# A fused low-rank update in fp16 on one core: A and B moved into SyncE's load queue, w laid out by ScalarE, stores released by turns

## The chip, the core and the metric

The kernel runs on one core of a Trainium2 chip. The metric is device time in microseconds. A profile shows one execution: the span from its first to its last instruction on the core, the busy times of the engines, and the transfers. PE is TensorE, DVE is VectorE, ACT is ScalarE, POOL is GpSimd and SP is SyncE, which only issues transfers here.

## What is computed

```python
batch, seq, d_model, r = 16, 512, 768, 16
x = np.random.randn(batch, seq, d_model).astype(np.float32)
A = np.random.randn(d_model, r).astype(np.float32) * 0.1
B = np.random.randn(r, d_model).astype(np.float32) * 0.1
scale = 0.5

def reference(x, A, B, scale):
    lora = np.matmul(np.matmul(x, A), B)
    return (x + scale * lora).astype(np.float32)
```

x and the output have 8192 rows of 768 fp32 numbers, 25.17 MB each. A and B have 48 KB each.

## The kernel before

The 8192 rows are 64 tiles of 128 rows. They are cut into six parts of 2, 6, 8, 16, 16 and 16 tiles (`PARTS`). Three rooms in SBUF of 16 tiles each (`rooms`) hold x; the last part takes the room of the first three parts again, so its two loads wait until the stores of those have landed. Seven transfers load x (`LOADS`, in tiles: 2, 6, 8, 16, 16, 8, 8) and seven with the same cuts store the result from the same place (`STORES`).

Work goes by groups of 8 tiles, eight in all, numbered here from 0. For each group:

1. ScalarE casts the first 4 tiles to fp16 into `xh` and GpSimd the other 4 (`narrowed`, L158).
2. VectorE turns each half in blocks of 32x32 (`turned`, L233), so that the 768 columns come to lie on partitions.
3. TensorE multiplies by `w_bd`, a layout of A, in 24 steps of 256 columns (`projected`, L261), into `y_ps`.
4. ScalarE scales the four blocks of the result into `y_bd` (`spread`, L197).
5. TensorE multiplies by `b_mm`, a layout of B, two tiles at a time (`raised`, L275), into the two PSUM buffers `lora`.
6. VectorE adds a pair of tiles of `lora` to x in place (L243), 4 additions a group. When the group is the last that a store needs, it drains and counts up `s_sum` (L247).

TensorE interleaves: group h's projection runs in three thirds, between the pairs of the group before. In its first round the pairs are empty runs, whose results nobody adds. VectorE turns group g+1 ahead of adding group g.

`xh`, `y_bd`, `y_ps` and `lora` have two buffers. Every engine has its own program, in the order written, and waits on semaphores. `s_free` counts lora buffers that VectorE has added, `s_lora` those that TensorE has filled, `s_y` finished projections.

The start: GpSimd clears `b_rows`, `pick`, `w_bd` and both `y_bd`; VectorE clears `a_rows` (L209). ScalarE issues the transfers of B (L180) and A (L184) on its own queue, each after the clearing of its target. ScalarE casts B (L189), TensorE spreads it over the partitions with `pick` (L285), and ScalarE copies the result to `b_mm` (L191). VectorE transposes A (L211), gathers it into `w_one` (L218, three copies) and copies that to the four diagonal blocks of `w_bd` (L226).

SyncE's program is the queue of x: five loads (L134), then the stores of parts 0 to 2 (L138), each after a wait on `s_sum`, then the last two loads, each after a wait for stores that have landed, then the other four stores.

Of the kernel before, what the change touches and what calls it, by code (L numbers as in the profile page):

```python
# [22 lines left out]
APART = 8  # L23
# [3 lines left out]
def kernel(  # L27
# [11 lines left out]
    Q = 32  # L39
    NQ = P // Q  # L40
# [4 lines left out]
    R = A.shape[1]  # L45
    NC = D // 64
    NG = sum(PARTS) // GROUP
    PAIRS = GROUP // 2
# [15 lines left out]
    a_rows = sb("a_rows", [P, 64 * R], fp32)  # L64
    a_t = sb("a_t", [P, 2, R, Q], fp32)
    w_one = sb("w_one", [Q, NC, 2, R], MM_DT)
    b_rows = sb("b_rows", [P, D], fp32)
    b_half = sb("b_half", [P, D], MM_DT)
    pick = sb("pick", [P, NQ, Q], MM_DT)
    w_bd = sb("w_bd", [P, NC, 2, P], MM_DT)  # L70
    b_mm = sb("b_mm", [P, D], MM_DT)
    xh = [sb(f"xh{i}", [P, GROUP, D], MM_DT) for i in range(2)]
    y_bd = [sb(f"y_bd{i}", [P, GROUP, P], MM_DT) for i in range(2)]
    lora = [ps(f"lora_ps{i}", [P, 2, D]) for i in range(2)]
# [4 lines left out]
    def sem(name):  # L79
        sems.append(nc.alloc_semaphore(name))  # L80
        return sems[-1]
# [18 lines left out]
    LOADS = [(0, 0, 2), (1, 0, 6), (2, 0, 8), (3, 0, 16), (4, 0, 16), (5, 0, 8), (5, 8, 8)]  # L100
# [5 lines left out]

    s_a, s_b = sem("s_a"), sem("s_b")
    s_brows, s_pick, s_bh, s_bp = sem("s_brows"), sem("s_pick"), sem("s_bh"), sem("s_bp")
    s_ready, s_zero, s_w, s_bm = sem("s_ready"), sem("s_zero"), sem("s_w"), sem("s_bm")
    s_nact, s_npool = sem("s_nact"), sem("s_npool")  # L110
    s_turned, s_y, s_spread = sem("s_turned"), sem("s_y"), sem("s_spread")
    s_lora, s_free, s_sum = sem("s_lora"), sem("s_free"), sem("s_sum")
# [18 lines left out]
    @block.sync  # L131
    def _(e):
        def load(ld):
            e.dma_start(out=held(*ld), in_=memory(x2, *ld)).then_inc(s_load[ld], 16)  # L134

        def store(st, done):
            e.wait_ge(s_sum, STORED.index(groups_for(*st)) + 1)
            e.dma_start(out=memory(out2, *st), in_=held(*st)).then_inc(done, 16)  # L138

        load(LOADS[0])  # L140
        for ld in LOADS[1:5]:
            load(ld)
        for st, done in zip(STORES, (s_out0, s_out0, s_out1)):
            store(st, done)
        e.wait_ge(s_out0, 32)
        load(LOADS[5])
        e.wait_ge(s_out1, 16)
        load(LOADS[6])
        for st in STORES[3:]:
            store(st, s_out)  # L150

    def narrowed(e, copy, done, g, q):
        t = g * GROUP + q * SUB
        for s in dict.fromkeys(load_sem(t + k) for k in range(SUB)):
            e.wait_ge(s, 16)
        if g >= 2:
            e.wait_ge(s_y, g - 1)
        copy(  # L158
            out=xh[g % 2][:, ds(q * SUB, SUB), :], in_=held(*where[t], SUB)
        ).then_inc(done, 1)  # L160

    @block.gpsimd
    def _(e):
        e.memset(b_rows, 0.0).then_inc(s_brows, 1)  # L164
        e.memset(pick, 0.0).then_inc(s_pick, 1)
        e.memset(w_bd.rearrange("p c k m -> p (c k m)").bitcast(fp32), 0.0)  # L166
        for t in y_bd:
            e.memset(t.rearrange("p s m -> p (s m)").bitcast(fp32), 0.0)  # L168
        e.wait_ge(s_pick, 1)
        e.affine_select(  # L170
            out=pick, in_=pick, compare_op=mybir.AluOpType.not_equal, fill=1.0, base=0,
            pattern=[[0, NQ], [-APART, Q]], channel_multiplier=1,
        ).then_inc(s_zero, 1)
        for g in range(NG):
            narrowed(e, e.tensor_copy, s_npool, g, 1)

    @block.scalar
    def _(e):
        e.wait_ge(s_brows, 1)
        e.dma_start(  # L180
            out=b_rows[0 : R * APART : APART, :], in_=B
        ).then_inc(s_b, 16)
        e.wait_ge(s_ready, 1)
        e.dma_start(  # L184
            out=a_rows[0 : NC * APART : APART, :],
            in_=A.rearrange("(c e) r -> c (e r)", e=64),
        ).then_inc(s_a, 16)
        e.wait_ge(s_b, 16)
        e.copy(out=b_half, in_=b_rows).then_inc(s_bh, 1)  # L189
        e.wait_ge(s_bp, 1)  # L190
        e.copy(out=b_mm, in_=lora[0][:, 0, :]).then_inc(s_bm, 1)  # L191

        def spread(g):
            e.wait_ge(s_y, g + 1)
            for b in range(NQ):
                q = ds(b * Q, Q)
                last = e.mul(out=y_bd[g % 2][q, :, q], in_=y_ps[g % 2][q, :, :], mul=sc)  # L197
            last.then_inc(s_spread, 1)

        narrowed(e, e.copy, s_nact, 0, 0)  # L200
        narrowed(e, e.copy, s_nact, 1, 0)
        for g in range(NG):
            spread(g)
            if g + 2 < NG:
                narrowed(e, e.copy, s_nact, g + 2, 0)

    @block.vector
    def _(e):
        e.memset(a_rows, 0.0).then_inc(s_ready, 1)  # L209
        e.wait_ge(s_a, 16)  # L210
        e.transpose(  # L211
            out=a_t[0 : NC * APART].rearrange("i k r c -> i (k r) c"),
            in_=a_rows[0 : NC * APART].rearrange("c (i k r) -> c (k r) i", k=2, r=R),
        ).then_inc(s_ready, 1)
        e.wait_ge(s_ready, 2)
        EACH = Q // APART
        for b in range(NC // EACH):
            last = e.tensor_copy(  # L218
                out=w_one[:, ds(b * EACH, EACH), :, :],
                in_=a_t[ds(b * Q, Q)].rearrange("i k r (c n) -> i c k r n", n=APART)[..., 0],  # L220
            )
        last.then_inc(s_ready, 1)
        e.wait_ge(s_ready, 3)
        e.wait_ge(s_zero, 1)
        for b in range(NQ):
            last = e.tensor_copy(out=w_bd[ds(b * Q, Q), :, :, ds(b * Q, R)], in_=w_one)  # L226
        last.then_inc(s_w, 1)

        def turned(g):
            for q, s in ((0, s_nact), (1, s_npool)):  # L230
                e.wait_ge(s, g + 1)
                v = xh[g % 2][:, ds(q * SUB, SUB), :].bitcast(fp32)
                last = e.transpose(out=v, in_=v)  # L233
            last.then_inc(s_turned, 1)

        turned(0)
        for g in range(NG):
            if g + 1 < NG:
                turned(g + 1)
            for p in range(PAIRS):  # L240
                xs = held(*where[g * GROUP + 2 * p], 2)
                e.wait_ge(s_lora, (g + 1) * PAIRS + p + 1)
                e.tensor_tensor(  # L243
                    out=xs, in0=xs, in1=lora[p % 2], op=mybir.AluOpType.add
                ).then_inc(s_free, 1)
            if g + 1 in STORED:
                e.drain().then_inc(s_sum, 1)  # L247

    @block.tensor
    def _(e):  # L250
        def take(s):
            e.wait_ge(s, 1)
            e.sem_inc(s, -1)  # L253

        def projected(h, steps):
            if steps[0] == 0:
                take(s_turned)
            xv = xh[h].rearrange("p s (c j k) -> p s c j k", c=NC, k=2)
            for m in steps:
                c, k = divmod(m, 2)  # L260
                last = e.matmul(  # L261
                    y_ps[h], w_bd[:, c, k, :], xv[:, :, c, :, k],
                    start=(m == 0), stop=(m == MMS - 1),
                )
            if steps[-1] == MMS - 1:
                last.then_inc(s_y, 1)

        def raised(h, p):
            if p == 0:
                take(s_spread)  # L270
            take(s_free)
            t = lora[p % 2]
            for k in range(2):
                for n0, w in ((0, 512), (512, 256)) if k == 0 else ((0, 256), (256, 512)):
                    last = e.matmul(  # L275
                        t[:, k, ds(n0, w)], y_bd[h][:, 2 * p + k, :], b_mm[:, ds(n0, w)],
                        start=True, stop=True,
                    )
            last.then_inc(s_lora, 1)


        e.wait_ge(s_bh, 1)
        e.wait_ge(s_zero, 1)
        for n0, w in ((0, 512), (512, 256)):
            last = e.matmul(  # L285
                lora[0][:, 0, ds(n0, w)], pick.rearrange("p b r -> p (b r)"),
                b_half[:, ds(n0, w)], start=True, stop=True,
            )
        last.then_inc(s_bp, 1)
        e.sem_inc(s_spread, 1)  # L290
        e.sem_inc(s_free, 2 + PAIRS)
        e.wait_ge(s_w, 1)
        e.wait_ge(s_bm, 1)
        with e.Fori(0, NG // 2):
            for h in range(2):
                raised(1 - h, 0)
                raised(1 - h, 1)
                projected(h, range(0, THIRD))
                raised(1 - h, 2)
                projected(h, range(THIRD, 2 * THIRD))  # L300
                raised(1 - h, 3)
                projected(h, range(2 * THIRD, MMS))
        for p in range(PAIRS):
            raised(1, p)
# [43 lines left out]
```

## Time and profile before

| what | value |
|---|---|
| time, median of 3 runs | 124.71 us (124.66 to 126.03) |
| profiled execution | 124.84 us, its span 122.93 us |
| busy: VectorE | 87.0 us, 71% of the span |
| busy: TensorE matmuls / weight loads | 53.9 us / 31.8 us |
| busy: ScalarE / GpSimd | 36.9 us / 25.6 us |
| moved | 50.46 MB, 410 GB/s over the span |
| queue q1 (SyncE's) | 50.33 MB, 96.5% of 16 DMA engines' span |
| queue q10 (ScalarE's) | 0.10 MB, 0.2% |
| B, issue to landing | 6.9 us |
| mean granted TensorE clock | 0.899 |

Times in the timeline count from the first instruction of the span. A group's line gives the code line, engine, operation, output and inputs with their shapes, how many there were, the busy time and the mean of one, and the idle time before them with what ended it. A wait of several semaphores is put down to the one that came last. In a table of stretches, a packet is booked in the stretch in which it starts or ends, so the DMA share of a short stretch can be over 1.

### The profile page before, as it was taken

To read this page: it belongs to the slowest core of one execution; us is meant where nothing else is said; L and a number is where in the kernel's file an instruction comes from. 1 tells how busy PE (TensorE), PEld (TensorE's weight loads), DVE (VectorE), ACT (ScalarE), POOL (GpSimd) and SP (SyncE) were. 2 spreads that over 40 slices of the span, in tenths; PEclk is the share of its full clock that TensorE was granted. 3 is DMA by queue.
4 is the path that set the end of the run, shared out by engine and by line. 5 is a ranking of instruction groups with operands and counts; after the bars stand their busy time and mean duration, and the time that the engine had idled before them with its cause. 6 is when DMAs were issued, how large, how long until landed. Compare 5 with 4: busy or idle time off the path is not lost. (4 is left out here: it accounts for less than half of the span.)

```text
span 122.9 us, 967 instructions
## 1 busy us (share of the span) xinstructions
PE 53.9 (44%) x338; PEld 31.8 (26%) x338; DVE 87.0 (71%) x57; ACT 36.9 (30%) x43; POOL 25.6 (21%) x18
## 2 busy tenths in 40 slices
PE   0002068768306994493483477449438353000000
PEld 0000034445103562262242254236225221000000
DVE  2006993959729989999999999999999789300000
ACT  0416608220199106708504082640400400000000
POOL 7402608000196001708000080440000000000000
PEclk9999999999995599999999999999999999555555
DMA  3999999799799795999999999999899799799990
GB/s 98 429 415 450 416 528 432 336 512 480 304 496 496 320 464 228 490 418 432 456 392 464 432 400 480 400 496 448 352 480 496 336 464 466 325 456 400 456 440 40
DMA packets 2074, 50.46 MB, mean 410 GB/s; under 512 B 252, under 2 KB 252, under 8 KB 536
## 3 DMA queue, kind: packets, MB, share of 16 engines
q1 hardware_dynamic: 2016, 50.33, 96.5%
q10 hardware_dynamic: 56, 0.10, 0.2%
q8 instruction: 1, 0.02, 0.0%
q14 instruction: 1, 0.01, 0.0%
HBM read 25.26 MB, written 25.17 MB: 410 GB/s over the span
## 5 line engine op out<-in xcount | busy, mean ns | idle before, releaser
L243 DVE TENSOR_TENSOR x_sb<-x_sb,lora_ps 128x1536 f32<-128x1536 f32 x32 | 53.8, 1740 | 3.5 <-PE lora_ps L275 3.5
L275 PE MATMUL lora_ps<-b_mm,y_bd 128*128 128x512 f16 (+1 forms) x144 | 30.9, 351 | 30.8 <-PEq L253 30.8
L158 POOL CAST xh<-x_sb 128x3072 f16<-128x3072 f32 x8 | 21.9, 2746 | 55.0 <-DMA x_sb<-in_x_dram 50.5
L233 DVE STREAM_TRANSPOSE xh<-xh 128x1536 f32<-128x1536 f32 x16 | 27.5, 1755 | 5.4 <-ACT xh L158 5.0
L261 PE MATMUL ps_yt<-xh,w_bd 128*128 128x256 f16 x192 | 26.1, 277 | 9.0 <-PEq L253 9.0
L158 ACT CAST xh<-x_sb 128x3072 f16<-128x3072 f32 x8 | 22.0, 2752 | 18.2 <-DMA x_sb<-in_x_dram 18.2
L275 PEld LDWEIGHTS lora_ps<-b_mm,y_bd 128*128 128x128 f16 x144 | 13.2, 102 | 44.6 <-issue 38.9
L261 PEld LDWEIGHTS ps_yt<-xh,w_bd 128*128 128x128 f16 x192 | 18.4, 98 | 16.9 <-issue 12.0
L197 ACT ACTIVATE y_bd<-ps_yt 32x256 f16<-32x256 f32 x32 | 12.0, 374 | 34.3 <-PE ps_yt L261 34.0
L211 DVE STREAM_TRANSPOSE a_t<-a_rows 96x1024 f32<-96x1024 f32 x1 | 1.9, 1926 | 8.3 <-DMA a_rows<-in_A_dram 8.3
L285 PE MATMUL lora_ps<-b_half,pick 128*128 128x512 f16 (+1 forms) x2 | 0.8, 514 | 9.6 <-ACT b_half L189 9.6
L285 PEld LDWEIGHTS lora_ps<-b_half,pick 128*128 128x128 f16 x2 | 0.1, 110 | 9.6 <-ACT b_half L189 9.6
L218 DVE CAST w_one<-a_t 32x128 f16<-32x128 f32 x3 | 2.5, 836 | 0.1
L189 ACT ACT_TABLE_LOAD x1 | 1.3, 1283 | 3.7 <-issue 3.7
L189 ACT CAST b_half<-b_rows 128x768 f16<-128x768 f32 x1 | 0.8, 832 | 3.7 <-DMA b_rows<-in_B_dram 3.7
L209 DVE MEMSET a_rows<- 128x1024 f32 x1 | 0.9, 912 | 1.2 <-SPq L127 1.2
L166 POOL MEMSET w_bd<- 128x1536 f32 x1 | 1.4, 1382 | 0.0
L191 ACT CAST b_mm<-lora_ps 128x768 f16<-128x768 f32 x1 | 0.8, 798 | 0.9 <-PE lora_ps L285 0.9
L226 DVE COPY w_bd<-w_one 32x384 f16<-32x384 f16 x4 | 1.0, 251 | 0.1
L168 POOL MEMSET y_bd<- 128x512 f32 x2 | 1.0, 524 | 0.0
L164 POOL MEMSET b_rows<- 128x768 f32 x1 | 0.7, 737 | 0.5 <-SPq L127 0.5
L170 POOL TENSOR_SCALAR_AFFINE_SELECT pick<-pick 128x128 f16<-128x128 f16 x1 | 0.3, 309 | 0.0
(5 smaller groups left out, 0.6 us busy)
## 6 DMA issues: line engine op xcount, KB each, us to landing
x_sb<-in_x_dram SPq DMA_DIRECT2D x2, 6144.0 KB, 38.1
out_dram<-x_sb SPq DMA_DIRECT2D x2, 6144.0 KB, 22.9
x_sb<-in_x_dram SPq DMA_DIRECT2D x3, 3072.0 KB, 15.1
out_dram<-x_sb SPq DMA_DIRECT2D x3, 3072.0 KB, 16.4
x_sb<-in_x_dram SPq DMA_DIRECT2D x1, 2304.0 KB, 10.1
out_dram<-x_sb SPq DMA_DIRECT2D x1, 2304.0 KB, 22.3
x_sb<-in_x_dram SPq DMA_DIRECT2D x1, 768.0 KB, 4.5
out_dram<-x_sb SPq DMA_DIRECT2D x1, 768.0 KB, 17.2
```

The costliest lines, as they stand in the source:

```text
L158: copy(out=xh[g % 2][:, ds(q * SUB, SUB), :], in_=held(*where[t], SUB)).then_inc(done, 1)
L166: e.memset(w_bd.rearrange("p c k m -> p (c k m)").bitcast(fp32), 0.0)
L168: e.memset(t.rearrange("p s m -> p (s m)").bitcast(fp32), 0.0)
L189: e.copy(out=b_half, in_=b_rows).then_inc(s_bh, 1)
L197: last = e.mul(out=y_bd[g % 2][q, :, q], in_=y_ps[g % 2][q, :, :], mul=sc)
L211: e.transpose(out=a_t[0 : NC * APART].rearrange("i k r c -> i (k r) c"), in_=a_rows[0 : NC * APART].rearrange("c (i k r) -> c (k r) i", k= ...
L218: last = e.tensor_copy(out=w_one[:, ds(b * EACH, EACH), :, :], in_=a_t[ds(b * Q, Q)].rearrange("i k r (c n) -> i c k r n", n=APART)[..., 0],)
L226: last = e.tensor_copy(out=w_bd[ds(b * Q, Q), :, :, ds(b * Q, R)], in_=w_one)
L233: last = e.transpose(out=v, in_=v)
L243: e.tensor_tensor(out=xs, in0=xs, in1=lora[p % 2], op=mybir.AluOpType.add).then_inc(s_free, 1)
L261: last = e.matmul(y_ps[h], w_bd[:, c, k, :], xv[:, :, c, :, k], start=(m == 0), stop=(m == MMS - 1),)
L275: last = e.matmul(t[:, k, ds(n0, w)], y_bd[h][:, 2 * p + k, :], b_mm[:, ds(n0, w)], start=True, stop=True,)
```

## The change

Six edits come together.

- SyncE issues the transfers of A and then B behind the second load of x, each after the wait for its cleared target, and then the third load. ScalarE issues none.
- GpSimd clears `a_rows`, 96 partitions of it and as its first work, in VectorE's place. It also does the first counting up of `s_spread` and `s_free`, which TensorE did.
- ScalarE copies `w_one` into the four blocks of `w_bd`, after its cast of group 0, then copies `b_mm`. VectorE did the former, and ScalarE did the latter ahead of that cast. ScalarE's order makes the semaphore `s_w` unnecessary, and TensorE waits for neither `s_w` nor `s_zero`.
- TensorE takes both `lora` buffers ahead of a group's first pair, and none ahead of the second.
- The stores of parts 0 to 3 are released by VectorE's first turn that follows the group's additions in its program, in place of a drain. For the stores after groups 5 and 6 the drain stays; the last store is released by the last addition itself.
- ScalarE's casts from group 2 on don't wait for `s_y`, which ScalarE has waited for in `spread` already.

```diff
@@ SyncE
         load(LOADS[0])
-        for ld in LOADS[1:5]:
+        load(LOADS[1])
+        e.wait_ge(s_ready, 1)
+        e.dma_start(
+            out=a_rows[0 : NC * APART : APART, :], in_=A.rearrange("(c e) r -> c (e r)", e=64)
+        ).then_inc(s_a, 16)
+        e.wait_ge(s_brows, 1)
+        e.dma_start(out=b_rows[0 : R * APART : APART, :], in_=B).then_inc(s_b, 16)
+        for ld in LOADS[2:5]:
             load(ld)
...
@@ narrowed
-        if g >= 2:
+        if q and g >= 2:
             e.wait_ge(s_y, g - 1)
...
@@ GpSimd
+        e.memset(a_rows[0 : NC * APART], 0.0).then_inc(s_ready, 1)
         e.memset(b_rows, 0.0).then_inc(s_brows, 1)
+
+        e.sem_inc(s_spread, 1)
+        e.sem_inc(s_free, 2 + PAIRS)
...
@@ ScalarE
-        e.wait_ge(s_brows, 1)
-        e.dma_start(
-            out=b_rows[0 : R * APART : APART, :], in_=B
-        ).then_inc(s_b, 16)
-        e.wait_ge(s_ready, 1)
-        e.dma_start(
-            out=a_rows[0 : NC * APART : APART, :],
-            in_=A.rearrange("(c e) r -> c (e r)", e=64),
-        ).then_inc(s_a, 16)
+        e.wait_ge(s_zero, 1)
         e.wait_ge(s_b, 16)
         e.copy(out=b_half, in_=b_rows).then_inc(s_bh, 1)
-        e.wait_ge(s_bp, 1)
-        e.copy(out=b_mm, in_=lora[0][:, 0, :]).then_inc(s_bm, 1)
...
         narrowed(e, e.copy, s_nact, 0, 0)
+        e.wait_ge(s_ready, 3)
+        for b in range(NQ):
+            e.copy(out=w_bd[ds(b * Q, Q), :, :, ds(b * Q, R)], in_=w_one)
+        e.wait_ge(s_bp, 1)
+        e.copy(out=b_mm, in_=lora[0][:, 0, :]).then_inc(s_bm, 1)
         narrowed(e, e.copy, s_nact, 1, 0)
...
@@ VectorE
-        e.memset(a_rows, 0.0).then_inc(s_ready, 1)
...
-        e.wait_ge(s_ready, 3)
-        e.wait_ge(s_zero, 1)
-        for b in range(NQ):
-            last = e.tensor_copy(out=w_bd[ds(b * Q, Q), :, :, ds(b * Q, R)], in_=w_one)
-        last.then_inc(s_w, 1)
...
-                last = e.transpose(out=v, in_=v)
-            last.then_inc(s_turned, 1)
+                ins = e.transpose(out=v, in_=v)
+                if q:
+                    ins.then_inc(s_turned, 1)
+                elif g - 1 in STORED[:-3]:
+
+                    ins.then_inc(s_sum, 1)
...
-                e.tensor_tensor(
+                ins = e.tensor_tensor(
                     out=xs, in0=xs, in1=lora[p % 2], op=mybir.AluOpType.add
-                ).then_inc(s_free, 1)
-            if g + 1 in STORED:
+                )
+                if g + 1 < NG or p + 2 < PAIRS:
+                    ins.then_inc(s_free, 1)
+                elif p + 1 == PAIRS:
+                    ins.then_inc(s_sum, 1)
+            if g + 1 in STORED[-3:-1]:
                 e.drain().then_inc(s_sum, 1)
...
@@ TensorE
-        def take(s):
-            e.wait_ge(s, 1)
-            e.sem_inc(s, -1)
+        def take(s, n=1):
+            e.wait_ge(s, n)
+            e.sem_inc(s, -n)
...
             if p == 0:
                 take(s_spread)
-            take(s_free)
+                take(s_free, 2)
+            elif p > 1:
+                take(s_free)
...
-
         e.wait_ge(s_bh, 1)
-        e.wait_ge(s_zero, 1)
...
-        e.sem_inc(s_spread, 1)
-        e.sem_inc(s_free, 2 + PAIRS)
-        e.wait_ge(s_w, 1)
         e.wait_ge(s_bm, 1)
```

`STORED` is [1, 2, 4, 6, 7, 8]: the numbers of finished groups at which a store can go.

## The prediction

> **What bounds the kernel now.** I read the page's slices and queues first, then a table of long stretches, then the DMA queue's own waits, then the timeline of the start and of the groups.
>
> The slices and the queues:
>
> ```profile
> DMA  3999999799799795999999999999899799799990
> GB/s 98 429 415 450 416 528 432 336 512 480 304 496 496 320 464 228 490 418 432 456 392 464 432 400 480 400 496 448 352 480 496 336 464 466 325 456 400 456 440 40
> ...
> q1 hardware_dynamic: 2016, 50.33, 96.5%
> q10 hardware_dynamic: 56, 0.10, 0.2%
> ```
>
> The 16 DMA engines are busy from the first slice to the last, and 96.5% of the whole span belongs to one queue, q1, which is SyncE's: loads and stores of x. q10 is ScalarE's queue; its 0.10 MB are A and B. Single slices scatter because a packet is booked whole, so I took long stretches (columns: length, the five engines' busy time, clock, DMA share, GB/s):
>
> ```profile
> 22.00:42.00 20.00, 11.52 (x70) 6.97 (x69) 15.65 (x10) 8.50 (x10) 5.44 (x2) 0.86 1.00 433
> 43.00:48.00 5.00, 3.09 (x23) 2.07 (x22) 4.25 (x3) 1.50 (x4) 0.00 (x0) 0.96 0.95 338
> 49.00:119.00 70.00, 31.36 (x211) 18.55 (x208) 55.08 (x33) 18.10 (x24) 10.62 (x4) 0.90 1.01 433
> 106.00:118.00 12.00, 0.00 (x0) 0.00 (x0) 0.00 (x0) 0.00 (x0) 0.00 (x0) 0.50 1.00 430
> ```
>
> The rate is 430 to 433 GB/s whether all engines work (22 to 42, 49 to 119) or none does (106 to 118). So the DMA engines are at their rate and compute does not slow them. The floor follows: 50.43 MB / 0.432 = 116.7 us, plus 2.0 before the first packet (the first load is issued at 0.94, and the stretch 1 to 2 us moves 18 GB/s), plus 1.9 after the last (121 to 122.93 moves nothing), plus the 1.9 by which the profiled execution's 124.84 exceeds its span of 122.93. That makes 122.5. Only 2.3 us of 124.84 are loss inside the transfers, and 5 x (1 - 338/432) = 1.1 of them lie in the stretch 43 to 48, where the queue turns from loads to stores.
>
> What the queue's issuer waits for (columns: waiter, line, releaser, us in total, times, longest):
>
> ```profile
> SPq L138 <- DVEq L247: 83.2, 6, 29.3
> SPq L134 <- DMA out_dram<-x_sb: 15.6, 2, 8.6
> ```
>
> SyncE waits 83 us for VectorE's drain after a group (L247), and still the queue never runs dry: those are waits of the issuer, with earlier transfers still queued. The chain that ended last accounts for 7% of the span and stops at the last store's issue at 105.7, 16 us before its data is out; it is not what sets the end. What sets it is when q1 starts and whether it ever empties.
>
> **The change, part by part.** For each part the question is: does q1 start later, carry more, or run empty?
>
> *A and B move to q1.* Their bytes go with them, 96 KB, 0.23 us at 432 GB/s, so total traffic is the same. They used to be taken between x's packets (B landed 6.9 us after its issue), now they stand behind 768 + 2304 KB. SyncE also issues them ahead of the third load. Five x loads took 2.98 us to issue; on ScalarE the B issue took 0.62 and the A issue 1.30. Both waits are for GpSimd memsets: b_rows took 0.74 from 0.94, a_rows (1024 elements, now first) scales to 0.98. So a_rows is ready at 1.9, b_rows at 2.7, and the third load is issued at about 2.2 + 1.3 + 0.6 = 4.1 instead of some 2. Cover: the first two loads keep q1 busy until load 1 lands at 11.5; without it, a late issue would cost its lateness one for one. Behind this wait stand loads 2 to 4 and all stores. I price it at 0. What no row shows is whether two small transfers inside q1 open a gap. Lower bound -0.3 (x's packets are no longer interrupted by q10's: the stretch 2 to 12 ran at 404 instead of 432 GB/s, 0.6 us, of which at most half can be theirs). Upper bound: load 0 lands 4.5 us after its issue, 1.8 of that is its data, so 2.7 us is what a transfer costs standing alone; two are 5.3. I take -0.1, because seven x transfers follow each other in this queue at full rate with different sizes, which is the nearest row.
>
> The Trainium skill, "DMA: Bandwidth & Descriptors" (Anatomy of one DMA; Rules for kernel authors), speaks against the change here: about 2.0 us fixed per transfer, and under 64 KB mostly overhead. Taken as time of the queue, that estimate is +4.0, or 128.6 us. The trace has the 2.7 for load 0 but no gap behind it, so I read the fixed part as latency that the next transfer covers.
>
> *The weights come later, and ScalarE lays out w_bd.* The rows of the start:
>
> ```profile
> 10.39 1.93 DVE L211 STREAM_TRANSPOSE a_t<-a_rows 96x1024 f32<-96x1024 f32 x1 [8.25 <-DMA a_rows<-in_A_dram]
> 11.49 2.74 POOL L158 CAST xh<-x_sb 128x3072 f16<-128x3072 f32 x1 [7.08 <-DMA x_sb<-in_x_dram]
> 12.36 2.54 DVE L218 CAST w_one<-a_t 32x128 f16<-32x128 f32 x3
> 14.92 1.04 DVE L226 COPY w_bd<-w_one 32x384 f16<-32x384 f16 x4
> 16.36 2.72 PE L275 MATMUL lora_ps<-b_mm,y_bd 128*128 128x512 f16 x8 [5.97 <-PEq L253]
> 19.58 1.05 PE L261 MATMUL ps_yt<-xh,w_bd 128*128 128x256 f16 x8 [0.51 <-PEq L253]
> ```
>
> Load 1 lands at 11.5, so A and B land at about 11.7 (before: 10.4 and 8.7). VectorE then has 1.93 + 2.54, to 16.2, and its first turn starts 0.2 later than the 16.00 of before. ScalarE: b_half 0.83 to 12.5, the first cast 2.75 to 15.3, then it waits for w_one until 16.2. The four w_bd copies on ScalarE have no row: bounds are 0.25 each (VectorE's same copy) and 0.83 (ScalarE's 128x768 cast); its 32x256 activation took 0.374, and on the line to 832 at 768 elements 384 give 0.49. Four are 2.0, to 18.2; b_mm 0.80, to 19.0. Behind these stands group 1's cast (L158), which starts at 19.0 instead of 18.76. TensorE starts at 19.0 instead of 16.36, 2.7 later, and the first projection (19.58) moves by 2.2 to 2.7, since its other input, the turned tile, was ready at 19.4 anyway. What is late next is group 0's four additions, which ended at 33.18: now 35.4 to 35.9. The stall ends here:
>
> ```profile
> 33.30 2.75 ACT L158 CAST xh<-x_sb 128x3072 f16<-128x3072 f32 x1 [8.01 <-DMA x_sb<-in_x_dram]
> 36.08 3.44 DVE L233 STREAM_TRANSPOSE xh<-xh 128x1536 f32<-128x1536 f32 x2 [2.90 <-ACT xh L158]
> 47.16 3.44 DVE L233 STREAM_TRANSPOSE xh<-xh 128x1536 f32<-128x1536 f32 x2
> 67.35 3.44 DVE L233 STREAM_TRANSPOSE xh<-xh 128x1536 f32<-128x1536 f32 x2
> ```
>
> All three compute engines wait for load 3 at 33.3; VectorE idles 2.90 us until 36.08, and 2.2 to 2.7 disappear in it. At the upper bound for the copies (1.4 more) VectorE would be up to 1.2 late from there. 0 in the sum, as long as no store is late.
>
> *Stores released by turns.* Stores 0 and 1 go out after the first of the two turns at 36.08, at 37.8 instead of 33.26; q1 is then busy with loads until about 47. Store 2 goes after the first turn at 47.16, at 48.9 instead of 47.4; q1 then has stores 0 and 1, which land at 56.0. Store 3 goes at 67.35 + 1.7 = 69.1 instead of 67.3; loads 5 and 6 fill q1 until 78.5. Behind SyncE's wait for store 2 stands load 5, which waits for stores 0 and 1 anyway. Stores 4 to 6 keep their points. The tightest is store 4: issued at 87.5, while q1 has store 3 until 78.5 + 14.5 = 93.0. So VectorE may be 5.5 us late before any microsecond is lost. Price 0; without this cover store 2 alone would cost 1.5.
>
> *Shorter programs.* TensorE takes both lora buffers before pair 0 instead of one. Group 2's first pair starts at 47.91, after the additions that end at 47.03, and at 97.99 after 97.6: no new wait. The dropped semaphore steps, drains and ScalarE's wait on s_y lie on engines that have these 5.5 us to spare, and the memset of a_rows leaves VectorE while it waits for A. 0 each.
>
> **Sum.** 124.84 - 0.1 = 124.7 for an execution like the profiled one; that one is 0.1 above the median of 124.71, so I forecast a median of 124.6. Own range of this case: 123.9 to 125.4.
>
> **Rivals.** (1) *The small transfers break q1 open.* Place: between load 1 and load 2, at 11 us. If q1 waits for A's and B's latency, it loses up to 2.7 each: 124.7 + 5.3 = 130.0. It decides from 1.25 us each on, where the time is 2.5 us up (2%). For it: no small transfer has yet run in this queue, and the turn at 43 to 48 shows that q1 can lose 1.1 us at a boundary. Against: no boundary between two loads shows a loss. (2) *The weights are much later.* If A landed with load 2 (18.7) instead of 11.7, 7 more us push group 0's additions to 42.7, 6.6 past 36.08; less the 5.5 of cover, store 4 is some 1.1 us late and store 2, at 55.5, up to 1: 126.8. Against it, A and B stand ahead of load 2. (3) *The loss at the turn goes.* If stores queued at 37.8 are taken without the 1.1 us and x is no longer interrupted: 124.6 - 1.1 - 0.3 = 123.2. Nothing shows that the moment of issue, 9 instead of 13 us ahead of the turn, matters to it. (4) *The change reaches nothing*: programs shrink where nobody waits, A and B cost in q1 what they cost in q10: 124.8, which can hardly be told from the forecast.
>
> **How the numbers follow.** Forecast with (4): 0.70; (3): 0.09; (2): 0.06; (1): 0.15. A measurement of this kernel can tell about 2% (2.5 us) from no change. Faster by that means under 122.2, below the floor of 122.5, so only an error of mine in the floor gives it: 0.05, out of (3). Slower: (1) beyond its point 0.14 and the far end of (2) 0.03, together 0.17. Same: 0.78. The range leaves out the far side of (1) and the best of (3): 123.2 to 127.0.
>
> **What would show it.** q1 with about 50.43 MB and q10 gone; about 432 GB/s from 12 us on; ScalarE's w_bd copies near 0.5 us each; TensorE's first L275-type matmul near 19; VectorE's idle time before the turn at 36 shrunk from 2.90 to under 1; stores issued at 38, 49 and 69. Wrong would be a stretch near 11 or after 48 well under 430 GB/s, or SyncE's store waits ending with an empty queue.

## The result and the profile after

The changed kernel takes 125.52 us (median of 22 runs) where the kernel before, run beside it, takes 124.78: a ratio of 1.0048 with a 95% interval of 1.0028 to 1.0069. It is slower by half a per cent, far less than 2%, but clear of zero. The profiled execution took 125.52 us, with a span of 123.45. Times and ratios leave out slow runs, more than 1.5% above the fastest of their kernel; in all that follows only the kernel `dve_minus2` has any, two of twelve.

The page's slices and queues of the kernel after:

```profile
DMA  3999999699899996999999999899989979899990
GB/s 92 438 448 432 398 518 478 287 510 494 350 430 510 462 303 269 446 416 494 398 430 454 390 462 526 350 462 478 414 382 494 462 334 478 366 430 451 398 398 16
...
q1 hardware_dynamic: 2072, 50.43, 96.2%
q8 instruction: 1, 0.02, 0.0%
```

q10 is gone, and its 56 packets and 0.10 MB stand in q1. The long stretches (columns as before the prediction):

```profile
2.00:12.00 10.00, 0.00 (x0) 0.00 (x0) 1.03 (x1) 0.29 (x1) 3.77 (x7) 1.00 1.00 402
22.00:42.00 20.00, 14.94 (x91) 9.17 (x90) 15.53 (x10) 8.51 (x10) 5.44 (x2) 0.91 1.00 433
43.00:48.00 5.00, 3.13 (x23) 1.89 (x22) 5.00 (x4) 1.50 (x4) 0.00 (x0) 1.00 0.93 323
49.00:119.00 70.00, 33.65 (x208) 19.85 (x208) 54.59 (x33) 18.21 (x24) 10.72 (x4) 0.86 1.01 434
```

The long ones read as before, 402 for 404, 433 for 433, 434 for 433; the short stretch 43 to 48 has 323 for 338. The packet records of the trace say it outright: from the first packet of x to the last it took 119.72 us before and 119.72 us after, and that last packet ended 121.68 and 121.70 us into the span. This is one execution of each kernel, and that they agree to 0.01 us is partly luck: spans of the kernel before run from 122.4 to 124.0 us. In these two executions nothing that moves data became slower. The tail, from the end of the last packet to the end of the span, is 1.25 us before the change and 1.75 us after it. The loss lies behind the last byte.

There the engines meet in two last barriers, where each waits until all have arrived. Rows of the line that closes the program, first of the kernel before (columns: engine's sequencer, operation, count, shortest/median/longest in ns, first and last start):

```profile
L343 DVEq DRAIN  x2: 10/10/10, 106.6 to 122.6; - x2
...
L343 DVEq EVENT_SEMAPHORE  x2: 21/21/21, 122.5 to 122.9; - x2
```

and of the kernel after:

```profile
L348 DVEq DRAIN  x2: 10/72/134, 107.8 to 123.1; - x2
...
L348 DVEq EVENT_SEMAPHORE  x2: 21/21/21, 122.6 to 123.4; - x2
```

VectorE leaves the last barrier but one at 122.5 and 122.6. Its next instruction, a drain with no work of VectorE ahead of it, follows in 0.11 us before (122.451 to 122.563 in the instruction records) and in 0.51 after (122.588 to 123.100), and it takes 134 ns where it took 10. That is a stop of 0.40 us with nothing to wait for, and the last barrier waits for it. SyncE's waits (waiter, releaser, us in total, times, longest) show the same delay. Before, and then after:

```profile
SPq L343 <- PEq L343: 0.5, 2, 0.4
```

```profile
SPq L348 <- PEq L348: 0.9, 2, 0.7
```

The longest wait grew from 0.4 to 0.7. The row names TensorE, but TensorE's own drain there started at 122.74, before VectorE's. When the engine named had long been done, the releaser was another.

### The profile page after: what moved, and what is told of

The parts are those of the page before. It is cut to its first block, busy times and chain, and to the rows that moved or that the text cites. A ratio compares the mean times of both kernels' runs of the same rounds, so it can differ in the third digit from the quotient of the medians.

```text
span 123.5 us, 946 instructions
## 1 busy us (share of the span) xinstructions
PE 56.3 (46%) x338; PEld 33.0 (27%) x338; DVE 84.5 (68%) x52; ACT 38.7 (31%) x47; POOL 26.5 (21%) x19
## 3 DMA queue, kind: packets, MB, share of 16 engines
q1 hardware_dynamic: 2072, 50.43, 96.2%
## 5 line engine op out<-in xcount | busy, mean ns | idle before, releaser
L285 PE MATMUL lora_ps<-b_mm,y_bd 128*128 128x512 f16 (+1 forms) x144 | 31.6, 358 | 26.3 <-PEq L261 26.3
L269 PE MATMUL ps_yt<-xh,w_bd 128*128 128x256 f16 x192 | 28.0, 291 | 7.9 <-PEq L261 7.9
L285 PEld LDWEIGHTS lora_ps<-b_mm,y_bd 128*128 128x128 f16 x144 | 13.5, 104 | 40.6 <-issue 34.9
L269 PEld LDWEIGHTS ps_yt<-xh,w_bd 128*128 128x128 f16 x192 | 19.4, 103 | 16.5 <-issue 10.8
L204 ACT COPY w_bd<-w_one 32x384 f16<-32x384 f16 x4 | 2.0, 508 | 0.0
L223 DVE CAST w_one<-a_t 32x128 f16<-32x128 f32 x3 | 2.0, 657 | 0.1
L171 POOL MEMSET a_rows<- 96x1024 f32 x1 | 0.9, 948 | 0.5 <-SPq L127 0.5
## 6 DMA issues: line engine op xcount, KB each, us to landing
x_sb<-in_x_dram SPq DMA_DIRECT2D x2, 6144.0 KB, 36.6
```

The lines of the kernel that those rows point to most:

```text
L204: e.copy(out=w_bd[ds(b * Q, Q), :, :, ds(b * Q, R)], in_=w_one)
L223: last = e.tensor_copy(out=w_one[:, ds(b * EACH, EACH), :, :], in_=a_t[ds(b * Q, Q)].rearrange("i k r (c n) -> i c k r n", n=APART)[..., 0],)
L269: last = e.matmul(y_ps[h], w_bd[:, c, k, :], xv[:, :, c, :, k], start=(m == 0), stop=(m == MMS - 1),)
L285: last = e.matmul(t[:, k, ds(n0, w)], y_bd[h][:, 2 * p + k, :], b_mm[:, ds(n0, w)], start=True, stop=True,)
```

## The experiments

Theory T says that VectorE's program, ten instructions shorter (70 in the compiled program for 80; 65 instruction records in the trace for 75, which leaves the plain branches out), puts a boundary of its instruction stream into the final barriers. Its rivals are that A and B in q1 cost the time (Q), and that fewer steps on VectorE or later stores and weights do.

**One instruction more, and ten.**

```diff
     @block.vector
     def _(e):
+        for _ in range(1):              # dve_plus10: range(20)
+            e.wait_ge(s_brows, 1)
         e.wait_ge(s_a, 16)
```

Two such waits are packed into one instruction, so 20 of them make ten.

> The changed kernel with one more instruction at the head of VectorE's program: a wait on b_rows's clearing, which ends at 2.6 us, while VectorE waits for A until 11 us anyway. Theory T (the tail): the loss lies behind the last byte. q1 moves the same bytes in the same 119.72 us in both kernels, but in the changed one VectorE passes the last barrier but one 0.54 us later than before (a stop of 0.4 us between two instructions there), because the shorter program puts some boundary of its instruction stream on that very place; one more instruction moves the boundary to an instruction that stands in the 14 us wait for the last stores. T expects span minus last packet back from 1.75 to some 1.3 us, a span near 123.0 and a time of 124.9 to 125.1, about 0.5 under the changed kernel. Theory Q (A and B in q1, or the later weights, cost it): the time stays at 125.5.

> The changed kernel with ten more such waits at the head of VectorE's program, so that it has as many instructions as before (80 in the compiled program, 70 in the changed kernel). T expects the same as with one more: no stop of VectorE in the last barriers, a time of 124.8 to 125.1. If it were the one wait itself and not the place that helps, ten would differ from one. Q: 125.5.

With one: 125.08 us, 1.0038 (1.0009 to 1.0067). With ten: 125.17 us, 1.0024 (1.0006 to 1.0041). The stop is gone in both. VectorE's row of the closing line and SyncE's wait, with one more instruction:

```profile
L350 DVEq DRAIN  x2: 10/14/17, 107.6 to 122.6; - x2
```

```profile
SPq L350 <- PEq L350: 0.5, 2, 0.4
```

The tail is 1.37 and 1.34 us instead of 1.75. An instruction added at the head of a program, where it costs nothing, took 0.4 us off the tail, as T has it. The times fit less well. With one the median is where T had it, with ten it is just above T's 125.1. The medians are 0.44 and 0.35 us under the changed kernel's, which was measured in another set of runs, but the intervals of the ratios overlap with its own (1.0028 to 1.0069): the tail settles this, the time alone does not. Over the kernel before in the same set (124.88) 0.2 and 0.3 us are left by the medians, 0.5 and 0.3 by the ratios.

**A and B, undone alone and done alone.**

```diff
# after_ab_scalar: the changed kernel, SyncE
-        e.wait_ge(s_ready, 1)
-        e.dma_start(out=a_rows[...], in_=A...).then_inc(s_a, 16)
-        e.wait_ge(s_brows, 1)
-        e.dma_start(out=b_rows[...], in_=B).then_inc(s_b, 16)
# ScalarE: the two issues of the kernel before, ahead of its wait on s_zero
# before_ab_sync: the kernel before with these four lines moved the other way
```

> The changed kernel with one part undone: ScalarE issues B and A on its own queue again, as before; VectorE's and TensorE's programs are those of the changed kernel. T expects the stop in the last barrier to stay and the time at 125.5 (125.3 to 125.7). Q expects the loss to go: 124.7 to 124.9.

> The kernel before with one part done: SyncE issues A and B behind x's second load, all else as before. T expects no loss: 124.6 to 124.9, q1 at 50.43 MB in some 119.7 us, and no stop of VectorE in the tail. Q expects the whole loss: 125.4 to 125.6.

Undone in the changed kernel: 125.36 us, 1.0063 (1.0039 to 1.0087), and VectorE's stop is there (drain of 135 ns, a tail of 1.73). Done alone in the kernel before: 124.61 us, 0.9982 (0.9960 to 1.0003), no stop, a tail of 1.25. Moving A and B costs nothing; if it does anything, it gains 0.2 us. Q falls as to A and B. These runs also show how little the times and spans over all runs can tell of 0.4 us: `after_ab_scalar`, with the stop, and the two kernels with one and ten instructions more, without it, were measured in one set, and the median span of all three is 123.15 us.

**One instruction less, and two.** The releases of the last stores go from drains to instructions that are there anyway.

```diff
-                elif g - 1 in STORED[:-3]:
+                elif g - 1 in STORED[:-2]:
...
-            if g + 1 in STORED[-3:-1]:
+            if g + 1 in STORED[-2:-1]:     # dve_minus2: no drain at all,
                 e.drain().then_inc(s_sum, 1)
# dve_minus2: the third addition of the last group counts up s_sum too
```

> The changed kernel with VectorE's last two drains taken out as well (68 instructions instead of 70): the store after group 5 is released by the first turn of group 7, the store after group 6 by the third addition of group 7. In the changed kernel the stop stands ahead of VectorE's last instruction but one, number 69 of 70. T expects the stop to move past the last instruction of the span: span minus last packet back at 1.2 to 1.4 us and the span near 123.0; whether the time follows (125.0) or the stop is paid behind the span (125.4) it can't say. Theory R (fewer steps on VectorE is what hurts, or drains help the stores): 125.5 or more, with the tail as long as in the changed kernel.

> The changed kernel with one of VectorE's two drains taken out (69 instructions): the store after group 5 is released by the first turn of group 7. T expects the stop of 0.4 us still inside the span, now ahead of the very last instruction: span minus last packet 1.65 to 1.8, time 125.4 to 125.6. Theory R: the same or more; apart from the run with two out, it tells nothing on R.

With one less: 125.35 us, 1.0037 (1.0007 to 1.0067). The stop moved by one instruction, as T has it: VectorE's very last instruction follows 0.50 us behind its drain (123.431 to 123.933) instead of 0.31. The tail is 1.52, less than the 1.65 expected, because 0.31 us of that gap is the wait for the others in any case; the time is just under the 125.4 expected. With two less, the span has no stop and a tail of 1.36. The time does not follow: 125.75 us (124.80 to 126.25 in ten runs), 1.0068 (1.0034 to 1.0103). So it disagrees with both figures that T gave, and it meets the "125.5 or more" of theory R, whose tail "as long as in the changed kernel" it does not meet. Against the kernel before in the same set, it is 1.1 us longer: by the medians some 0.3 outside the span (2.23 for 1.93), which could be the stop paid there, and 0.9 inside (123.6 for 122.7). What makes these 0.9 is not known, and R is not excluded as their cause.

**The stop put into the kernel before.**

```diff
         e.memset(a_rows, 0.0).then_inc(s_ready, 1)
+        for _ in range(108):               # before_plus118: range(236)
+            e.wait_ge(s_brows, 1)
         e.wait_ge(s_a, 16)
```

> The kernel before with 54 more instructions at the head of VectorE's program, waits on b_rows's clearing, while it waits for A: 134 in all, 64 more than the changed kernel's 70. Nothing else is touched, and 54 of these waits are over before A lands. If T is right and the boundary comes back every 64 instructions, the stop appears in the last barriers of the kernel before: span minus last packet 1.65 to 1.8 instead of 1.25, time 125.1 to 125.3 instead of 124.8. If the boundaries lie further apart, or if T is wrong, nothing changes: 124.6 to 124.9.

> The kernel before with 118 more waits at the head of VectorE's program (198 instructions, 128 more than the changed kernel's 70). With 54 more the tail stayed at 1.24 us, so boundaries are not 64 apart; the instruction transfers on q14 are of 8192 bytes, which at 64 bytes an instruction (what a spacing of 128 would make) puts the next boundary where the changed kernel has its own. T with 128 expects VectorE's stop in the last barriers of the kernel before: span minus last packet 1.6 to 1.8. If the boundaries are further apart, or there is no such thing: 1.2 to 1.3. In time: the run with 54 more was at 125.9 with its extra instruction transfer at 16 us; T expects 0.3 to 0.5 above that, 126.2 to 126.4, the other 125.7 to 126.1.

With 54 more (134 instructions), no stop in the tail: the boundaries are not 64 apart. With 118 more (198), the stop appears in the kernel before, where nothing but these waits was added. They run until 13.5 us, past A's landing, so that VectorE turns A at 13.61 instead of 10.39. The same two rows:

```profile
L345 DVEq DRAIN  x2: 10/60/111, 106.6 to 124.4; - x2
```

```profile
SPq L345 <- PEq L345: 0.9, 2, 0.7
```

The drain follows 0.50 us after the release (123.929 to 124.424), and the tail is 1.58, just short of the range. The same run shows the boundary ahead of that. The added waits follow each other every 0.098 us, except that record 63 of VectorE (its instruction records in order of start, counted from 0) comes 0.49 us after record 62 (7.376 to 7.867). The late drain at the end is record 191, 128 further. In the changed kernel the late drain is record 63 as well; with one drain less it was the last instruction, again record 63; with two less, the last record is 62 and there was no stop to see. So the stop of 0.38 to 0.40 us stands ahead of record 63, and in the one program long enough to show it, again 128 later. Behind running work nothing shows of it: with 54 more, record 63 is a copy that starts 0.03 us after the cast ahead of it ended (14.844 after 14.809). After the stop an instruction transfer of 8192 bytes runs on q14: 0.7 us after the late drain where the DMA engines are idle (123.10 and 123.80 in the changed kernel), 3.6 us after it beside x's loads (7.87 and 11.50). In the kernel before, record 63 is an addition, and this transfer is the one on q14 in its list of queues, which the kernel after has no longer inside its span:

```profile
q14 instruction: 1, 0.01, 0.0%
```

The Trainium skill, "Runtime: NRT & Kernel Launch" (Instruction fetch mechanics), describes this: an engine streams its program in blocks by its own DMA queue, and crossing a boundary costs one bump of the queue's tail, "mostly hidden". The trace agrees on the transfer and gives the price where it isn't hidden, 0.4 us. The page has blocks of 256 instructions and 16 KiB; for VectorE the trace shows 128 records and transfers of 8192 bytes, and the measurement decides. That the bump is what VectorE does in these 0.4 us is the page's account; the runs show only the place, the spacing and the transfer.

The times: 125.90 us (1.0076, 1.0048 to 1.0105) with 54 more, which was to be 124.6 to 124.9. It has no stop in the tail, but its last packet ended at 122.78 instead of 121.68 us. With 118 more the time is 126.26 us (four runs; 1.0106, 1.0072 to 1.0139), 0.36 above that and in T's range; but its last packet ended at 123.17, 0.39 later too, so the time is no evidence for the stop here. The tail is. The packet records show where the 1.1 and 1.5 us come from. The stream as a whole is not slower: 50 of the 50.43 MB had gone at 120.22 us in the kernel before, at 120.14 with 54 more and at 120.23 with 118. At the end two packets of 24,576 bytes, 0.91 us each, stand one behind the other while the others are done: they run from 120.96 to 122.78 where all else had ended by 121.14, and from 121.35 to 123.17 where all else had ended by 121.56. In the kernel before, the last packet ended 0.26 us behind all others. Both programs have VectorE's instruction transfer early in the load stream, at 16 and 11.5 us instead of 102, but that is not needed for it: `dve_minus1`, whose transfer lies behind the span, also ends on two such packets (120.61 to 122.43, all else by 121.30). Why they are left over stays open.

**What is left over.** Three runs undo one more part each, two of them with VectorE's program longer by that very part.

```diff
# after_drains (VectorE 73): drains after groups 0, 1, 3, 5, 6, no release by turns
-            if g + 1 in STORED[-3:-1]:
+            if g + 1 in STORED[:-1]:
# after_w_vector (75): VectorE copies w_bd, ScalarE copies b_mm ahead of its first cast
# after_pe_back (71): TensorE's program as before, and one wait more on VectorE
```

> The changed kernel with the release of stores undone: drains after groups 0, 1 and 3 instead of turns (VectorE has 73 instructions). With one and with ten more instructions 0.2 to 0.3 us over the kernel before were left (1.0038 and 1.0024), while A and B in q1 alone cost nothing (0.9982). T alone, where the rest is scatter or lies elsewhere: no stop in the tail, 125.0 to 125.2. If the later stores (38, 49 and 69 us instead of 33, 47 and 67) are the rest: 124.6 to 124.8.

> The changed kernel with the laying out of w undone: VectorE copies w_bd again and ScalarE copies b_mm ahead of its first cast (VectorE has 75 instructions). T: no stop in the tail (1.2 to 1.4), a time of 124.7 to 125.1, under the changed kernel. If the later weights were what is left over after the stop is removed, 124.6 to 124.8 against the 125.1 and 125.2 of the kernels with one and ten instructions more; if they have no part in it, 124.9 to 125.2.

> The changed kernel with TensorE's program as before (lora buffers taken one at a time, its own counting up, the wait on s_zero), and one more wait at the head of VectorE's, which takes the stop out of the tail. If TensorE's shorter program holds the 0.2 to 0.3 us that one more instruction left over the kernel before, 124.6 to 124.9. If not, 125.0 to 125.2 as with the one instruction alone. Theory T says only that the tail is 1.2 to 1.4.

In this order: 124.91 us, 1.0011 (0.9984 to 1.0038); 124.88 us, 1.0000 (0.9980 to 1.0020); 124.92 us, 1.0012 (0.9988 to 1.0035). Each of these times lies between the figures that its expectation gave for the two readings. None has the stop in the last barriers (with the drains back, record 63 is a drain at 107.5 that took 142 ns, in the wait for the last stores, where it costs nothing), and none can be told from the kernel before. Nor can they be told from the two with one and ten instructions more (1.0038 and 1.0024), whose intervals they overlap; so these runs don't put the rest down to stores, weights or TensorE. On the whole the time goes with the tail, but not in every pair. These three and the two with one and ten instructions more, all without the stop, lie between 1.0000 and 1.0038, middle 1.0012; the three with the stop in the span at 1.0037 (`dve_minus1`), 1.0048 (the changed kernel) and 1.0063 (`after_ab_scalar`). `dve_minus2`, without it in the span, is at 1.0068 and speaks against it.

One more trait ran through the traces. The last landing came 0.33 to 0.34 us after the last packet in some kernels and 0.42 to 0.45 in the others.

```diff
# before_pool_count: the kernel before
@@ GpSimd
         e.memset(b_rows, 0.0).then_inc(s_brows, 1)
+        e.sem_inc(s_spread, 1)
+        e.sem_inc(s_free, 2 + PAIRS)
@@ TensorE
-        e.sem_inc(s_spread, 1)
-        e.sem_inc(s_free, 2 + PAIRS)
```

> The kernel before with one more part done: GpSimd does the first counting up of s_spread and s_free, in TensorE's place. In five kernels that have TensorE's program and this counting as before, the last landing is recorded 0.33 to 0.34 us after the end of the last packet; in eight that have the counting on GpSimd and the shorter program of TensorE, 0.42 to 0.45. If the counting is what makes that 0.1, this kernel shows 0.42 to 0.45, and its time is 0.1 over the kernel before, which a ratio can hardly show (1.001). If it is TensorE's way of taking the buffers, it shows 0.33 to 0.34 and 1.000. Theory T has no part in it: VectorE has 80 instructions and no stop in the tail either way.

It shows 0.43 us and a tail of 1.34, and 124.78 us with a ratio of 0.9995 (0.9974 to 1.0017). The counting on GpSimd goes with the later landing, 0.1 us, and with a tail that is as much longer, but the time doesn't show it. Why it should be later isn't known.

## Why the prediction was wrong

The forecast was 124.6 us, 0.1 below the run of before. Measured were 125.52, 0.74 above the median of before; the ratio makes it 0.6. The kernel became slower where it was to become a little faster, and the time lies outside the case's own 123.9 to 125.4.

*The step that failed* is "Shorter programs", priced at 0 each. It asked which instructions went and whether their engines had time to spare, and they had: 5.5 us, of which 0.45 was used. It did not ask where the rest of the program then came to lie. The sum took 1.9 us after the last packet, up to the end of the span, and another 1.9 outside it as fixed, and compared only what lies between. In the two profiled executions, the last packet's end moved by 0.02 us and the tail by 0.50. Of this, 0.40 is VectorE's stop, shown in the tail by moving it out, one place on and into the kernel before; 0.1 is the later last landing. Over all runs the median span is 123.45 us, against 122.7 to 123.0 in the four sets of runs of the kernel before that list their spans (median times 124.65 to 124.88), and what lies outside the span is 2.02 against 1.93. So the larger part, 0.45 to 0.75 us, is inside the span, where the stop is. That the median time pays exactly these 0.50 us is not shown, and the remaining 0.1 to 0.2 is not put down to a part of the change.

The 1.9 itself was misread. The table of stretches books a packet whole, and shows nothing after 121, though the last packets, begun before that, ended as late as 121.68. The tail of the kernel before was 1.25. The loss inside the transfers was then 119.72 - 116.7 = 3.0 us instead of 2.3. The forecast doesn't hang on this, since it only adds -0.1 to the profiled time.

*q1* was read rightly, and it decided the size: all six edits together left the stream at 119.72 us in the profiled execution. The price of -0.1 for A and B in q1, out of bounds of -0.3 and +5.3, fits the run that does this alone (0.9982, 0.9960 to 1.0003). Rival (1) is excluded with it. The estimate of +4.0 that went with the Trainium skill, "DMA: Bandwidth & Descriptors" (Anatomy of one DMA), is not borne out as time of the queue; that section fits its 2.0 us to transfers issued by GpSimd, and these are issued by SyncE. Rivals (2) and (3) didn't come either: A's transpose started at 10.97, and the stretch 43 to 48 still runs at 323 GB/s. Rival (4), no change, is wrong by the same 0.6.

*The start* was right in mechanism and too low in size. The line of ScalarE's table load in the kernel before, and then the timeline of the kernel after:

```profile
3.70 1.28 ACT L189 ACT_TABLE_LOAD   x1 [3.70 <-issue]
```

```profile
10.97 1.93 DVE L216 STREAM_TRANSPOSE a_t<-a_rows 96x1024 f32<-96x1024 f32 x1 [10.97 <-DMA a_rows<-in_A_dram]
...
11.71 1.28 ACT L192 ACT_TABLE_LOAD   x1 [11.71 <-DMA b_rows<-in_B_dram]
...
13.00 0.83 ACT L192 CAST b_half<-b_rows 128x768 f16<-128x768 f32 x1
...
16.39 2.07 ACT L204 COPY w_bd<-w_one 32x384 f16<-32x384 f16 x4
...
19.65 2.72 PE L285 MATMUL lora_ps<-b_mm,y_bd 128*128 128x512 f16 x8 [4.95 <-PEq L261]
...
22.16 1.90 PE L269 MATMUL ps_yt<-xh,w_bd 128*128 128x256 f16 x8
...
29.86 6.75 DVE L247 TENSOR_TENSOR x_sb<-x_sb,lora_ps 128x1536 f32<-128x1536 f32 x4 [4.47 <-PE lora_ps L285]
...
36.53 3.43 DVE L233 STREAM_TRANSPOSE xh<-xh 128x1536 f32<-128x1536 f32 x2
```

The w_bd copies took 0.51 us each, where 0.49 was interpolated between ScalarE's rows. What the prediction missed is ScalarE's table load. Before, it ran at 3.70 while ScalarE waited for B; now the wait on `s_b` stands ahead of it, and its 1.28 us come after B has landed. This goes with the added wait on `s_zero`, not with the move of A and B: the load runs at 0.91 in `before_ab_sync`, which has not this wait, and at 9.22, behind B's landing, in `after_ab_scalar`, which has it. A landed 0.7 us earlier than forecast, so the load's part is small: the `w_bd` copies started at 16.39 for 16.2, and the first projection at 22.16 is 2.6 us late, within the 2.2 to 2.7. Then its first eight matmuls took 1.90 us where they took 1.05 before, for which these runs show no cause. Group 0's additions ended at 36.6 instead of 35.4 to 35.9, and VectorE's turn at 36.08 came 0.45 us late. That was within the 5.5 us of cover, so it cost nothing.

*The stores* went out at 38.3, 48.3 and 69.1, for 37.8, 48.9 and 69.1 in the working (store 2 of the kernel before went out at 47.1, not 47.4), and q1 never ran empty, as forecast.

## What to carry to other kernels

In a kernel whose transfers fill the whole span, an edit on the engines is first a question of the two ends: what is issued before the first byte, and what stands after the last. Count the time from the last byte to the end separately, and look there for one engine that comes late with nothing to wait for. If a small slowdown lies there, add one harmless instruction at the head of that engine's program, and compare the tails of two profiles, because an effect of 0.4 us can drown in the scatter of the times: if the tail changes, it was the place of the code and not what the edit does.

## What the runs showed that was not expected

- VectorE stops for 0.38 to 0.40 us ahead of record 63 and again 128 records later, and an 8192-byte instruction transfer follows on q14. Inside a wait it is free; in the last barrier it made 0.40 of the 0.50 us by which the tail grew.
- An added wait that is already fulfilled costs VectorE 0.098 us from one to the next where it takes two semaphores (118 of them ran until 13.5 us).
- The semaphore counting on GpSimd instead of TensorE goes with a last landing that is 0.1 us later (0.43 for 0.34), with no cause that these runs show.
- The end of the stream is set by the last packets alone. In three kernels two packets of 0.91 us each were left over at the end, and the stream ended 0.7 to 1.5 us later though 50 MB had gone at the same time (120.1 to 120.4 us); why is not known.
